# A higher schedule priority for VectorE's operations between attention scores and the softmax

## The chip, the core and the metric

The kernel runs on one core of a Trainium2 chip. The metric is the device time of one execution in microseconds (us). TensorE is written PE, VectorE DVE, ScalarE ACT, GpSimd POOL, SyncE (which issues most transfers) SP.

## What is computed

Two layers of a hybrid decoder over 512 tokens of width 1024, all in float32. Each layer normalises its input, projects it with one matrix to eight parts, runs a gated linear recurrence (HGRN2) on one half and sliding-window attention with sinks on the other, gates both and projects back:

```python
h = rms_norm(x, g_pre)
q_h, f_h, i_h, z_h, q_a, k_a, v_a, z_a = split(h @ w_in)
o_h = rms_norm(hgrn2(q_h, f_h, i_h, lb), g_head) * silu(z_h)
o_a = sliding_window_attention(rotary(q_a), rotary(k_a), v_a, sinks) * silu(z_a)
x   = x + rms_norm(concat(o_h, o_a) @ w_out, g_post)
```

Attention has 16 query heads of 64 and 2 key/value heads. A block of 128 queries sees 128 keys back, so two key blocks. The softmax has one more term, the head's sink, in its denominator:

```python
s = where(mask, einsum('bnqkgd,bnskd->bnkgqs', qb, kw) * ATT_SCALE, NEG_INF)
p = softmax(concat([s, sink]))[..., :-1]
o = einsum('bnkgqs,bnskd->bnqkgd', p, vw)
```

## The kernel before

**Projections.** Weights come from HBM in pieces of 128x512 floats (SP, line 161). Each piece is split into a high part `whi` (a cast on ACT, line 181) and a low part `wlo` (a subtraction, mostly on DVE, line 182), and each product of the projections is three matmuls (L293): high by low, low by high, high by high, added up in one of three PSUM banks `pj`. `step()` emits three such matmuls at a time. It also emits conversions ahead of their use by a table of due steps; nine buffers hold converted pieces.

**Attention** is a second stream. `merge` interleaves it with the projection steps by weights, so that a piece of attention follows every few steps. It goes through 16 steps (four groups `g` of four heads by four query blocks `n`). A step starts with `att_scores`; `att_transpose` follows for the step two before, and `att_value` for the step four before. In `att_scores`:

- PE computes scores into a bank `sc`: one bank and eight matmuls for `n == 0` (L556), else two banks with four matmuls each (L567).
- DVE masks them in place (L559, or L571 for each bank), takes the maximum over keys (L560, or L572 for each bank), joins it with the sink to the negated maximum `negm` (L575) and computes the sink's difference `ds` (L577).
- ACT takes four exponentials with `negm` as bias, one per head, and their sums (L581), and one of `ds` (L584).
- DVE adds and inverts the sums (L585, L586); POOL multiplies (L588).

`att_transpose` turns the probabilities on PE into a bank `sc` (L594) and splits them into a high and a low part (ACT L339, DVE L340); POOL cuts them into two key blocks with `affine_select` (L606). `att_value` multiplies them with the values (PE L620, ACT L622, DVE L626). Three banks `sc` go round among scores and transposes (`SC = 3`): a score matmul may start when the exponentials, or L340, have read what its bank held. The rotation of queries also runs in this stretch: DVE L510 to L517 from the projection's bank, POOL L520 and L521, ACT L526, DVE L527, then a store and a load of the group's queries (SP L529 and L500).

**Order.** A scheduler orders each engine's instructions at build time: by when it takes them to be ready, and among ready ones by a priority that follows program order. `pin(...)` keeps pinned instructions in program order; the score matmuls are pinned, the operations on DVE here are not. `tc.high_priority(n)` makes what is emitted inside count as emitted n places earlier. Each engine's queue then runs in its built order, and an instruction that waits holds up all behind it.

Of the kernel before, what the change touches and what calls it, by code (L numbers as in the profile page):

```python
# [14 lines left out]
ALU = mybir.AluOpType  # L15
AX = mybir.AxisListType
# [8 lines left out]
SCALE = 1.0 / np.sqrt(64.0)  # L25
# [45 lines left out]
def hybrid_kernel(ctx: ExitStack, tc: tile.TileContext, x, wkv, win, wout, g_pre, g_post, lbp, ghead, sinks,  # L71
                  gcol_c, cos_f, sin_f, cos_t, sin_t, masks_c, out):
    nc = tc.nc
    P = 128
# [9 lines left out]
    def pin(ins):  # L84
        return tc.keep_in_program_order(ins)
# [8 lines left out]
    def sc():  # L94
        sc_turn[0] += 1
        return sc_tiles[sc_turn[0] % SC]
# [5 lines left out]
    def tmp(tag, dt=F32, n=1):  # L102

        t = tp.tile([P, n, 512] if n > 1 else [P, 512], dt, tag=tag, name=tag, bufs=TB[tag])
        return t
# [337 lines left out]
    def layer(l, last):  # L443
# [98 lines left out]
        am4 = amask.unsqueeze(1).broadcast_to([P, 4, P])  # L542
        am2 = amask.unsqueeze(1).broadcast_to([P, 2, P])

        def att_scores(g, n):
            v = g // 2
            q = qs[g]
            hs = slice(4 * g, 4 * g + 4)
            t_ = slice(n * P, (n + 1) * P)
            mx_ = sm.tile([P, 4], F32, tag="mx", name="mx")  # L550
            cur = []
            if n == 0:
                S = sc()
                for h in range(4):
                    for p in range(2):
                        pin(nc.tensor.matmul(S[:, h * P:(h + 1) * P], lhsT=q[:, h, t_], rhs=kst[v][p][:, 0:P],  # L556
                                         start=(h == 0 and p == 0), stop=(h == 3 and p == 1)))
                Sv = S.rearrange("p (h s) -> p h s", h=4)
                nc.vector.copy_predicated(Sv, am4, neg.unsqueeze(2).broadcast_to([P, 4, P]))  # L559
                nc.vector.tensor_reduce(mx_, Sv, axis=AX.X, op=ALU.max)  # L560
                cur = [Sv[:, h, :] for h in range(4)]
            else:
                for hp_ in range(2):
                    S = sc()
                    for h in range(2):
                        for p in range(2):
                            pin(nc.tensor.matmul(S[:, h * 256:(h + 1) * 256], lhsT=q[:, 2 * hp_ + h, t_],  # L567
                                             rhs=kst[v][p][:, (n - 1) * P:(n + 1) * P],
                                             start=(h == 0 and p == 0), stop=(h == 1 and p == 1)))
                    Sv = S.rearrange("p (h s) -> p h s", h=2)  # L570
                    nc.vector.copy_predicated(Sv[:, :, P:2 * P], am2, Sv[:, :, 0:P])  # L571
                    nc.vector.tensor_reduce(mx_[:, 2 * hp_:2 * hp_ + 2], Sv[:, :, P:2 * P], axis=AX.X, op=ALU.max)  # L572
                    cur += [Sv[:, h, P:2 * P] for h in range(2)]
            negm = sm.tile([P, 4], F32, tag="negm", name="negm")
            nc.vector.scalar_tensor_tensor(negm, mx_, -SCALE, nsnk[:, l, hs], op0=ALU.mult, op1=ALU.min)  # L575
            ds_ = sm.tile([P, 4], F32, tag="ds", name="ds")
            nc.vector.tensor_tensor(ds_, snk[:, l, hs], negm, op=ALU.add)  # L577
            pt = tmp("s")
            sums = sm.tile([P, 4], F32, tag="sums", name="sums")
            for h in range(4):  # L580
                nc.scalar.activation(pt[:, h * P:(h + 1) * P], cur[h], AF.Exp, bias=negm[:, h:h + 1], scale=SCALE,  # L581
                                     accum_out=sums[:, h:h + 1])
            es = sm.tile([P, 4], F32, tag="es", name="es")
            nc.scalar.activation(es, ds_, AF.Exp)  # L584
            nc.vector.tensor_tensor(sums, sums, es, op=ALU.add)  # L585
            nc.vector.reciprocal(sums, sums)  # L586
            pv = pt.rearrange("p (h s) -> p h s", h=4)
            nc.gpsimd.tensor_tensor(pv, pv, sums.unsqueeze(2).broadcast_to([P, 4, P]), op=ALU.mult)  # L588
            return pt
# [38 lines left out]
        def att_stream(steps):  # L628


            pts, terms = {}, {}
            n = len(steps)
            for tt in range(NT):
                ensure(("k", l, tt))
            for i in range(n + VLAG):
                todo = []
                if i < n:
                    todo.append(lambda: pts.update({i: att_scores(*steps[i])}))
                if 2 <= i <= n + 1:
                    todo.append(lambda: terms.update({i - 2: att_transpose(*steps[i - 2], pts.pop(i - 2), i % 2)}))  # L640
                if i >= VLAG:
                    todo.append(lambda: att_value(*steps[i - VLAG], terms.pop(i - VLAG)))
                for fn in todo:
                    fn()
                    yield (SLOW[1] if i < SLOW[0] else 1.0) / len(todo)

                if i < n and steps[i][1] == NT - 1 and steps[i][0] < 2:
                    until(lambda: steps[i][0] + 2 in stacks)
                    load_q(steps[i][0] + 2)
# [431 lines left out]
    neg = const.tile([P, 1], F32, name="neg")  # L1081
    gh = const.tile([P, DEPTH], F32, name="gh")
    snk = const.tile([P, DEPTH, ATT_HEADS], F32, name="snk")
    nsnk = const.tile([P, DEPTH, ATT_HEADS], F32, name="nsnk")
# [95 lines left out]
```

## Time and profile before

| | us |
|---|---|
| median of 3 runs | 920.47 (920.27 to 921.49) |
| the profiled execution | 920.82 |
| its span, first to last instruction | 919.1 |

| engine | busy us | share of the span |
|---|---|---|
| PE, matmuls | 903.7 | 98% |
| PE, weight loads | 751.6 | 82% |
| DVE | 668.2 | 73% |
| ACT | 464.2 | 51% |
| POOL | 273.7 | 30% |

TensorE's granted clock was 0.999. Attention lies at about 60 to 165 us in layer 0 and 513 to 620 us in layer 1. A row of the timeline gives start, duration, engine, line, operation, tiles and count; in square brackets stands the idle time before it and who ended it. A line of the waits gives who waited for whom: microseconds in total, times, and the longest. In names, buffer numbers are left out. The shares are averages over the whole span; the stretches differ.

### The profile page before, as it was taken

The numbers are of one execution on the slowest core, as the hardware profiler recorded it, in microseconds if no ns is written. First come the engines' busy times: TensorE is split into PE (matmuls) and PEld (weight loads), VectorE is DVE, ScalarE is ACT, GpSimd is POOL, SyncE is SP. The second block draws the span as 40 slices with busy tenths as digits, with TensorE's granted clock in tenths as the row PEclk, the third lists the DMA queues.
The fourth block names the chain that finished last, engine by engine and source line by source line (L and its number), as shares of the span: only waits on it lengthen the run. The fifth ranks groups of instructions, "written<-read, shape, count | busy, mean of one in ns | idle before, by whom it ended". The sixth has DMA issues, their size and how long they took to land.

```text
span 919.1 us, 19004 instructions
## 1 busy us (share of the span) xinstructions
PE 903.7 (98%) x7240; PEld 751.6 (82%) x7240; DVE 668.2 (73%) x1326; ACT 464.2 (51%) x1100; POOL 273.7 (30%) x292
## 2 busy tenths in 40 slices
PE   8999999999999999999999999999999999999997
PEld 6888887888888888888888877888788888888885
DVE  5968877869854896655787689876889439866556
ACT  5535757652755422534464466686446463245242
POOL 3335443303413142121332254450134022330102
PEclk9999999999999999999999999999999999999999
DMA  6584612323222332333356557223322323213413
GB/s 225 184 241 135 166 38 86 92 84 102 71 70 69 121 99 73 92 103 115 116 165 190 161 148 173 58 70 92 94 71 82 93 78 95 82 47 93 138 35 137
DMA packets 56570, 100.74 MB, mean 110 GB/s; under 512 B 6560, under 2 KB 9120, under 8 KB 56480
## 3 DMA queue, kind: packets, MB, share of 16 engines
q1 hardware_dynamic: 56192, 99.40, 36.7%
q8 instruction: 57, 0.93, 0.4%
q14 instruction: 33, 0.27, 0.1%
q10 hardware_dynamic: 288, 0.14, 0.1%
HBM read 86.93 MB, written 12.58 MB: 108 GB/s over the span
## 4 chain that ended last, share of the span: by engine, by line
PE 88%; DVE 6%; ACT 2%; issue 1%; POOL 1%; DMA 0%; POOLq 0%; DVEq 0%; SPq 0%; ACTq 0%
PE pj L293 73%; PE sc L750 2%; PE sc L567 2%; PE ac L620 2%; PE ac L821 2%; DVE wlo L182 1%; PE ac L824 1%; PE ac L808 1%; ACT s L581 1%; PE sc L594 1%; PE sc L873 1%; PE sc L406 1%; PE sc L796 1%; DVE mx L572 0%; DVE a L340 0%
## 5 line engine op out<-in xcount | busy, mean ns | idle before, releaser
L182 DVE TENSOR_TENSOR wlo<-raw,whi 128x512 fp32r<-128x512 f32 x249 | 182.8, 748 | 51.4 <-ACT whi L181 50.6
L181 ACT CAST whi<-raw 128x512 fp32r<-128x512 f32 x256 | 154.2, 620 | 106.0 <-PE pj L293 92.7
L293 PE MATMUL pj<-hhi,wlo 128*128 128x512 f32 x512 | 203.7, 398 | 0.0
L293 PE MATMUL pj<-hhi,whi 128*128 128x512 f32 x512 | 199.7, 390 | 0.0
L293 PE MATMUL pj<-hlo,whi 128*128 128x512 f32 x512 | 199.5, 390 | 0.0
L293 PE MATMUL pj<-whi,ops 128*128 128x512 f32 (+1 forms) x520 | 172.5, 394 | 0.0
L293 PEld LDWEIGHTS pj<-hhi,whi 128*128 128x128 f32 x512 | 96.1, 188 | 20.7
L293 PEld LDWEIGHTS pj<-whi,ops 128*128 128x128 f32 x520 | 97.2, 188 | 19.3
L293 PEld LDWEIGHTS pj<-hhi,wlo 128*128 128x128 f32 x512 | 96.2, 188 | 19.1
L293 PEld LDWEIGHTS pj<-hlo,whi 128*128 128x128 f32 x512 | 96.3, 188 | 18.6
L293 PE MATMUL pj<-whi,hlo 128*128 128x512 f32 x256 | 103.5, 405 | 0.0
L293 PE MATMUL pj<-wlo,ops 128*128 128x512 f32 (+1 forms) x260 | 100.8, 388 | 0.0
L293 PE MATMUL pj<-wlo,hhi 128*128 128x512 f32 x256 | 100.4, 392 | 0.3 <-DVE wlo L182 0.2
L293 PE MATMUL pj<-whi,hhi 128*128 128x512 f32 x256 | 100.3, 392 | 0.0
L769 POOL TENSOR_TENSOR k<-k,tot 128x256 f32<-128x256 f32 x80 | 64.2, 832 | 107.1 <-PE sc L750 57.8
L581 ACT ACTIVATE s<-sc,negm 128x128 f32<-128x128 f32 x128 | 45.6, 368 | 38.7 <-DVE negm L575 38.7
L768 DVE TENSOR_TENSOR q<-q,tot 128x256 f32<-128x256 f32 x80 | 48.8, 648 | 12.7 <-PE sc L756 6.9
L293 PEld LDWEIGHTS pj<-whi,hhi 128*128 128x128 f32 x256 | 48.1, 188 | 10.2
L293 PEld LDWEIGHTS pj<-wlo,ops 128*128 128x128 f32 x260 | 49.0, 188 | 8.8
L293 PEld LDWEIGHTS pj<-wlo,hhi 128*128 128x128 f32 x256 | 48.3, 189 | 8.9 <-DVE wlo L182 1.0
L293 PEld LDWEIGHTS pj<-whi,hlo 128*128 128x128 f32 x256 | 48.2, 188 | 8.0
L588 POOL TENSOR_TENSOR s<-s,sums 128x512 f32<-128x512 f32 x32 | 34.1, 1067 | 44.3 <-DVE sums L586 28.6
(188 smaller groups left out, 1417.0 us busy)
## 6 DMA issues: line engine op xcount, KB each, us to landing
raw<-in_win_dram SPq DMA_DIRECT2D x192, 256.0 KB, 2.7
raw<-in_wout_dram SPq DMA_DIRECT2D x64, 256.0 KB, 2.7
stack<-rot SPq DMA_DIRECT2D x16, 512.0 KB, 3.4
qs<-stack SPq DMA_DIRECT2D x32, 256.0 KB, 4.7
a<-in_x_dram SPq DMA_DIRECT2D x12, 256.0 KB, 3.5
raw<-in_wkv_dram SPq DMA_DIRECT2D x8, 256.0 KB, 3.9
x_mid<-a SPq DMA_DIRECT2D x8, 256.0 KB, 2.8
a<-x_mid SPq DMA_DIRECT2D x8, 256.0 KB, 3.2
```

The source lines that it names most:

```text
L181: keep(nc.scalar.copy(hi, v))
L182: keep((nc.gpsimd if i in on_pool and i % 2 else nc.vector).tensor_tensor(lo, v, hi.bitcast(F32), op=ALU.subtract))
L293: nc.tensor.matmul(u.o, lhsT=u.sta(k, u.w)[i], rhs=u.mov(k, u.w)[j], start=(n == 0), stop=(n == len(u.list) - 1))
L406: pin(nc.tensor.transpose(o[:, j * P:(j + 1) * P], self.xn[:, c, j * P:(j + 1) * P], ident))
L567: pin(nc.tensor.matmul(S[:, h * 256:(h + 1) * 256], lhsT=q[:, 2 * hp_ + h, t_], rhs=kst[v][p][:, (n - 1) * P:(n + 1) * P], start=(h == 0 a ...
L581: nc.scalar.activation(pt[:, h * P:(h + 1) * P], cur[h], AF.Exp, bias=negm[:, h:h + 1], scale=SCALE, accum_out=sums[:, h:h + 1])
L588: nc.gpsimd.tensor_tensor(pv, pv, sums.unsqueeze(2).broadcast_to([P, 4, P]), op=ALU.mult)
L620: pin(nc.tensor.matmul(U, lhsT=vst[v][:, blk, :], rhs=d, start=(i == 0), stop=(i == len(terms) - 1)))
L750: pin(nc.tensor.matmul(L[32 * b:32 * b + 32, c:c + 16], lhsT=k[:, o_:o_ + 32], rhs=qv[:, blk:blk + qu, 1, :], start=True, stop=True, tile_ ...
L768: nc.vector.tensor_tensor(qv[:, :, 1, :], qv[:, :, 1, :], tv[:, :, 0].unsqueeze(2).broadcast_to([P, nb, hh]), op=ALU.mult)
L769: nc.gpsimd.tensor_tensor(kv_[:, :, 0, :], kv_[:, :, 0, :], tv[:, :, 1].unsqueeze(2).broadcast_to([P, nb, hh]), op=ALU.mult)
L821: pin(nc.tensor.matmul(O[:, c], lhsT=A[:, c], rhs=vs(j, n), start=(n == 0), stop=False))
```

## The change

Each of the six VectorE operations from the scores to the sink's difference is emitted with priority 300. No instruction is added or taken out, and no operand changes.

```diff
-                nc.vector.copy_predicated(Sv, am4, neg.unsqueeze(2).broadcast_to([P, 4, P]))
-                nc.vector.tensor_reduce(mx_, Sv, axis=AX.X, op=ALU.max)
+                with tc.high_priority(300):
+                    nc.vector.copy_predicated(Sv, am4, neg.unsqueeze(2).broadcast_to([P, 4, P]))
+                with tc.high_priority(300):
+                    nc.vector.tensor_reduce(mx_, Sv, axis=AX.X, op=ALU.max)
...
-                    nc.vector.copy_predicated(Sv[:, :, P:2 * P], am2, Sv[:, :, 0:P])
-                    nc.vector.tensor_reduce(mx_[:, 2 * hp_:2 * hp_ + 2], Sv[:, :, P:2 * P], axis=AX.X, op=ALU.max)
+                    with tc.high_priority(300):
+                        nc.vector.copy_predicated(Sv[:, :, P:2 * P], am2, Sv[:, :, 0:P])
+                    with tc.high_priority(300):
+                        nc.vector.tensor_reduce(mx_[:, 2 * hp_:2 * hp_ + 2], Sv[:, :, P:2 * P], axis=AX.X, op=ALU.max)
...
-            nc.vector.scalar_tensor_tensor(negm, mx_, -SCALE, nsnk[:, l, hs], op0=ALU.mult, op1=ALU.min)
+            with tc.high_priority(300):
+                nc.vector.scalar_tensor_tensor(negm, mx_, -SCALE, nsnk[:, l, hs], op0=ALU.mult, op1=ALU.min)
...
-            nc.vector.tensor_tensor(ds_, snk[:, l, hs], negm, op=ALU.add)
+            with tc.high_priority(300):
+                nc.vector.tensor_tensor(ds_, snk[:, l, hs], negm, op=ALU.add)
```

Lines shift: L559, L560, L571, L572, L575, L577 become L560, L562, L574, L576, L580, L583, and what follows moves by six (L581 is L587, L594 is L600, L626 is L632); L567 becomes L569. Below, numbers after a tile's name tell its bank (`sc_78` to `sc_80` are the three score banks). The order changes inside attention alone, in both layers. On PE it changes at five spots; on SP one weight load changes places with a query load in each layer.

*First place*, layer 0 at about 76 to 84 us, where the projection goes over to slab `IV`. DVE before:

```order
L340 TENSOR_TENSOR a<-sc_79,a 128x512
L517 TENSOR_TENSOR rot<-pj,cs 128x512
L571 COPY_PREDICATED sc_80<-masks,sc_80 128x2x128
L571 COPY_PREDICATED sc_78<-masks,sc_78 128x2x128
L572 TENSOR_REDUCE mx<-sc_80 128x2
L182 TENSOR_TENSOR wlo<-raw,whi 128x512
L572 TENSOR_REDUCE mx<-sc_78 128x2
L182 TENSOR_TENSOR wlo<-raw,whi 128x512 x2
L527 TENSOR_TENSOR rot<-rot 128x512 x2
L182 TENSOR_TENSOR wlo<-raw,whi 128x512
L575 SCALAR_TENSOR_TENSOR negm<-mx,nsnk 128x4
```

DVE now:

```order
L340 TENSOR_TENSOR a<-sc_79,a 128x512
L574 COPY_PREDICATED sc_80<-masks,sc_80 128x2x128
L574 COPY_PREDICATED sc_78<-masks,sc_78 128x2x128
L576 TENSOR_REDUCE mx<-sc_80 128x2
L576 TENSOR_REDUCE mx<-sc_78 128x2
L517 TENSOR_TENSOR rot<-pj,cs 128x512
L580 SCALAR_TENSOR_TENSOR negm<-mx,nsnk 128x4
L182 TENSOR_TENSOR wlo<-raw,whi 128x512
L583 TENSOR_TENSOR ds<-snk,negm 128x4
L182 TENSOR_TENSOR wlo<-raw,whi 128x512 x2
L527 TENSOR_TENSOR rot<-rot 128x512 x2
L182 TENSOR_TENSOR wlo<-raw,whi 128x512
```

The score operations and L517 now stand ahead of the first L182, and `negm` ahead of all four. ACT there, before and then now:

```order
L181 CAST whi<-raw 128x512 x3
L526 CAST rot<-rot 128x512 x2
L181 CAST whi<-raw 128x512
L339 CAST a<-sc_79 128x512
L657 COPY vt<-pj 128x512
L581 ACTIVATE s,sums<-sc_80,negm 128x128 x2
```

```order
L181 CAST whi<-raw 128x512 x2
L587 ACTIVATE s,sums<-sc_80,negm 128x128
L181 CAST whi<-raw 128x512
L526 CAST rot<-rot 128x512 x2
L181 CAST whi<-raw 128x512
L587 ACTIVATE s,sums<-sc_80,negm 128x128
```

The first exponential moved ahead of the third cast. In layer 1 ACT's order here is unchanged, and it had the exponential ahead of that cast before; on DVE only L517 moves behind the score operations there.

*Second place*, layer 0 at about 100 to 106 us, from group 1 to group 2; layer 1 moves alike. DVE before and then now:

```order
L182 TENSOR_TENSOR wlo<-raw,whi 128x512
L527 TENSOR_TENSOR rot<-rot 128x512 x2
L571 COPY_PREDICATED sc_79<-masks,sc_79 128x2x128
L571 COPY_PREDICATED sc_80<-masks,sc_80 128x2x128
L182 TENSOR_TENSOR wlo<-raw,whi 128x512
L572 TENSOR_REDUCE mx<-sc_79 128x2
L182 TENSOR_TENSOR wlo<-raw,whi 128x512
L572 TENSOR_REDUCE mx<-sc_80 128x2
L340 TENSOR_TENSOR a<-sc_78,a 128x512
L575 SCALAR_TENSOR_TENSOR negm<-mx,nsnk 128x4
```

```order
L574 COPY_PREDICATED sc_79<-masks,sc_79 128x2x128
L574 COPY_PREDICATED sc_80<-masks,sc_80 128x2x128
L576 TENSOR_REDUCE mx<-sc_79 128x2
L576 TENSOR_REDUCE mx<-sc_80 128x2
L182 TENSOR_TENSOR wlo<-raw,whi 128x512
L580 SCALAR_TENSOR_TENSOR negm<-mx,nsnk 128x4
L527 TENSOR_TENSOR rot<-rot 128x512
L583 TENSOR_TENSOR ds<-snk,negm 128x4
L527 TENSOR_TENSOR rot<-rot 128x512
L182 TENSOR_TENSOR wlo<-raw,whi 128x512 x2
L340 TENSOR_TENSOR a<-sc_78,a 128x512
```

Of three L182, two L527 and an L340 ahead of `negm`, one L182 is left. On PE, L556 of group 2 stands seven projection matmuls earlier, and six of these now stand between it and L594.

*Third place*, layer 0 at about 137 to 142 us; layer 1 moves alike. DVE before and then now:

```order
L571 COPY_PREDICATED sc_80<-masks,sc_80 128x2x128
L626 TENSOR_TENSOR oa<-ac_82,u 64x2x128
L182 TENSOR_TENSOR wlo<-raw,whi 128x512
L626 TENSOR_TENSOR oa<-ac_82,u 64x2x128
L572 TENSOR_REDUCE mx<-sc_80 128x2
L571 COPY_PREDICATED sc_78<-masks,sc_78 128x2x128
L182 TENSOR_TENSOR wlo<-raw,whi 128x512
L572 TENSOR_REDUCE mx<-sc_78 128x2
L340 TENSOR_TENSOR a<-sc_79,a 128x512
L575 SCALAR_TENSOR_TENSOR negm<-mx,nsnk 128x4
```

```order
L574 COPY_PREDICATED sc_80<-masks,sc_80 128x2x128
L632 TENSOR_TENSOR oa<-ac_82,u 64x2x128
L576 TENSOR_REDUCE mx<-sc_80 128x2
L574 COPY_PREDICATED sc_78<-masks,sc_78 128x2x128
L182 TENSOR_TENSOR wlo<-raw,whi 128x512
L576 TENSOR_REDUCE mx<-sc_78 128x2
L182 TENSOR_TENSOR wlo<-raw,whi 128x512
L580 SCALAR_TENSOR_TENSOR negm<-mx,nsnk 128x4
L632 TENSOR_TENSOR oa<-ac_82,u 64x2x128
L583 TENSOR_TENSOR ds<-snk,negm 128x4
L340 TENSOR_TENSOR a<-sc_79,a 128x512
```

L340 and the second half of the output sum (L626, now L632) fell behind `negm`.

## Prediction

> **What bounds the kernel now.** I read the page first, then who waited for whom, then the two attention stretches by windows, then the rows of single instructions.
>
> ```profile
> PE 903.7 (98%) x7240; PEld 751.6 (82%) x7240; DVE 668.2 (73%) x1326; ACT 464.2 (51%) x1100; POOL 273.7 (30%) x292
> PE 88%; DVE 6%; ACT 2%; issue 1%; POOL 1%; DMA 0%; POOLq 0%; DVEq 0%; SPq 0%; ACTq 0%
> ```
>
> TensorE (PE) is busy 98% of the span and makes 88% of the chain that ended last. An operation of VectorE (DVE) is worth time only where TensorE stands still for what follows from it. So the question is how long TensorE stands still in attention, and for whom.
>
> ```profile
> PEld sc L567 <- ACT s L581: 7.5, 16, 1.2
> PE sc L567 <- ACT s L581: 2.9, 5, 0.8
> ACT s L581 <- DVE negm L575: 38.7, 22, 6.3
> PE pj L293 <- DVE wlo L182: 0.2, 1, 0.2
> ```
>
> Read from below: a projection matmul (L293) waits for a weight's low part (wlo, L182) visibly once, for 0.2 us. The score matmuls (L567) wait 16 times for ScalarE's exponentials (L581), which must leave one of the three score banks first. The exponentials wait 22 times for the negated maximum (negm, L575), the end of the operations that get the priority.
>
> ```profile
> 105.00:120.00 15.00, 14.57 (x77) 11.69 (x76) 14.15 (x31) 9.62 (x36) 9.78 (x9) 1.00 0.79 181
> 135.00:150.00 15.00, 14.16 (x74) 11.24 (x72) 14.16 (x31) 11.02 (x36) 6.75 (x6) 1.00 0.36 98
> sum 105.00, PE 103.61 PEld 85.69 DVE 86.50 ACT 68.11 POOL 49.10; mean PE 14.80 PEld 12.24 DVE 12.36 ACT 9.73 POOL 7.01
> ```
>
> These are windows of layer 0's attention (length, then busy PE, PEld, DVE, ACT, POOL). Over 105 us DVE is busy 86.50, but where TensorE loses most, DVE is busy 14.15 and 14.16 of 15. There the order on DVE decides what is late. The visible idle, 105 - 103.61 = 1.4 us, is too small a sum: a matmul's row lasts longer than the step to the next one, so I take starts.
>
> ```profile
> 75.56 1.11 PE L567 MATMUL sc<-kst,qs 128*128 128x256 f32 x8
> 106.64 1.11 PE L556 MATMUL sc<-kst,qs 128*128 128x128 f32 x8
> 107.90 0.63 PE L594 MATMUL sc<-ident,s 128*128 128x128 f32 x4 [0.15 <-issue]
> 112.05 0.40 PE L293 MATMUL pj<-wlo,hhi 128*128 128x512 f32 x1
> 112.71 0.74 PE L567 MATMUL sc<-kst,qs 128*128 128x256 f32 x4 [0.27 <-ACT s L581]
> 117.64 1.41 PE L567 MATMUL sc<-kst,qs 128*128 128x256 f32 x8
> 141.38 0.39 PE L293 MATMUL pj<-hlo,whi 128*128 128x512 f32 x1
> 141.61 0.39 PE L293 MATMUL pj<-hhi,whi 128*128 128x512 f32 x1
> 142.79 1.44 PE L567 MATMUL sc<-kst,qs 128*128 128x256 f32 x8 [0.80 <-ACT s L581]
> 148.65 0.39 PE L293 MATMUL pj<-hhi,whi 128*128 128x512 f32 x1
> 149.08 1.45 PE L567 MATMUL sc<-kst,qs 128*128 128x256 f32 x8
> ```
>
> A projection matmul starts 0.23 after the last (141.38, 141.61), so 0.39 - 0.23 = 0.16 of each wait stays hidden. Eight score matmuls without a wait last 1.11. The stalls, with names for later: **P1** at 107.90, 0.15 + 0.16 = 0.31. **P2** at 112.71, 0.66 - 0.23 = 0.43. **P3** at 117.64, 1.41 - 1.11 = 0.30 (the second bank of the eight). **P4** at 142.79, 1.18 - 0.23 = 0.95, and 1.44 - 1.11 = 0.33 inside. **P5** at 149.08, 0.43 - 0.23 = 0.20, and 0.34 inside. Together 2.86 us; layer 1 has the same places 452.7 us later:
>
> ```profile
> 594.27 0.39 PE L293 MATMUL pj<-hhi,whi 128*128 128x512 f32 x1
> 595.45 1.44 PE L567 MATMUL sc<-kst,qs 128*128 128x256 f32 x8 [0.80 <-ACT s L581]
> ```
>
> P4 is again 1.18 - 0.23 = 0.95. Twice 2.86 = 5.7 us is all that this change can win.
>
> **The change, part by part.** No instruction is added or removed, so busy time on every engine stays; only waits move.
>
> *P4, the third place in the order.*
>
> ```profile
> 137.21 0.41 DVE L571 COPY_PREDICATED sc<-masks,sc 128x256 f32<-128x256 uint8 x1
> 137.53 0.40 DVE L626 TENSOR_TENSOR oa<-ac,u 64x256 f32<-64x256 f32 x1
> 139.54 0.43 DVE L572 TENSOR_REDUCE mx<-sc 128x2 f32<-128x256 f32 x1
> 140.21 0.69 DVE L182 TENSOR_TENSOR wlo<-raw,whi 128x512 fp32r<-128x512 f32 x1
> 141.15 0.68 DVE L340 TENSOR_TENSOR a<-sc,a 128x512 fp32r<-128x512 f32 x1
> 141.75 0.15 DVE L575 SCALAR_TENSOR_TENSOR negm<-mx,nsnk 128x4 f32<-128x4 f32 x1
> 141.93 0.37 ACT L581 ACTIVATE s<-sc,negm 128x128 f32<-128x128 f32 x1 [2.26 <-DVE negm L575]
> ```
>
> In the new order two L571, one L626, two L572 and two L182 stand before negm; L340 and the other L626 fall behind it. 2 x 0.41 + 0.40 + 2 x 0.43 + 2 x 0.69 = 3.46 from 137.21 gives 140.7 instead of 141.75: 1.1 earlier. TensorE wants the bank at 141.61 + 0.23 = 141.84 and got it 0.95 later, so this stall goes, and the 0.33 inside it: 1.28 won.
>
> *P5.* TensorE now comes 1.28 earlier. Between the sums of the step before and the next negm both orders hold the same amount (two L626, two operations of 0.69, the four score operations), so negm follows only the 1.1. P5 grows by 1.28 - 1.1 = 0.2. P4 and P5 together win 1.1; I take 1.0 for losses against GpSimd (POOL, below).
>
> *P1, P2, P3, the second place.*
>
> ```profile
> 105.39 0.15 DVE L575 SCALAR_TENSOR_TENSOR negm<-mx,nsnk 128x4 f32<-128x4 f32 x1
> ```
>
> Before it stood three L182, two L527, an L340; in the new order one L182. With the two L527, of L182's shape, at its 0.69, that is 4 x 0.69 + 0.68 = 3.4 earlier, so P1's bank is free. L556 of the next group stands seven matmuls (7 x 0.23 = 1.6 us) earlier on TensorE, so its maximum and exponentials can come 1.6 earlier against P2's 0.43 and P3's 0.30. I take all three as gone: 1.04.
>
> So 2.0 in each layer, 4.0 in all. Bounds: nothing (DVE is full there) and 5.7.
>
> *The first place.* Here the new order can cost time.
>
> ```profile
> 79.83 0.47 PE L293 MATMUL pj<-whi,hlo 128*128 128x512 f32 x1
> 80.43 0.50 PE L293 MATMUL pj<-wlo,hhi 128*128 128x512 f32 x1
> 78.94 2.04 DVE L182 TENSOR_TENSOR wlo<-raw,whi 128x512 fp32r<-128x512 f32 x2
> 78.09 1.74 POOL L521 TENSOR_TENSOR rot<-rot 128x512 f32<-128x512 f32 x1
> 64.16 1.29 POOL L521 TENSOR_TENSOR rot<-rot 128x512 f32<-128x512 f32 x1
> 531.87 0.50 PE L293 MATMUL pj<-wlo,hhi 128*128 128x512 f32 x1 [0.17 <-DVE wlo L182]
> 538.64 0.63 PE L567 MATMUL sc<-kst,qs 128*128 128x256 f32 x4
> 539.92 0.74 PE L567 MATMUL sc<-kst,qs 128*128 128x256 f32 x4 [0.65 <-ACT s L581]
> ```
>
> TensorE reads these weights as soon as they are made: it loses 0.60 - 0.23 = 0.37 at 80.43. The new order puts both L571, both L572 and L517 ahead of the first L182 here, and on ScalarE an exponential, which needs negm, ahead of the third cast. That is how layer 1 stands already before the change, and there this place costs 0.17 + 0.16 = 0.33 for the weight and 0.65 + 0.16 = 0.81 for the bank: 1.14. So layer 0 should lose 1.14 - 0.37 = 0.8. In layer 1 only L517 moves behind the score operations; L521 follows L517 and comes 4 x 0.4 = 1.6 later, beside the L182: between -0.3 and +0.8, I take 0.2, nearer to what layer 1 has.
>
> *What else moves.* L340, L626, L527 and L517 fall back by 1 to 3 us. L340's result is wanted on TensorE two steps later (one step is 149.08 - 142.79 = 6.3 us); L626 frees one of two accumulators; L517 a projection bank; the views name no wait of TensorE for any of the three. L527 feeds, through SP's queue, the queries of a group two groups on; behind it in that queue one weight load changes places with a query load. I cost these at nothing; without the cover each would cost its delay once. The other L182 are read later; the one visible wait of 0.2 us for a wlo says that they have room. If it is gone, that is the second rival.
>
> **Sum.** -4.0 + 0.8 + 0.2 = -3.0. The profiled execution took 920.82 (span 919.1), so 917.8; it lies 0.35 above the median of 920.47, against which it is 917.5. I say 917.7.
>
> **Rivals.** *DVE is simply full (no change).* P4 and P5 stay (1.8 per layer), P1 to P3 go (2.1 in all), the first place costs 0.8 in each layer: -0.5, about 920.3. For it: 14.16 of 15. Against it: L340 and L626 need not be done before negm. The Trainium skill ("Perfetto Trace Analysis", Optimization Strategy) holds that the same gap repeating on the engine that should be saturated can mean too little PSUM for the next tile. By that the three banks set the loss whatever the order, and the sum would be near zero; that P4 is 0.95 in both layers agrees, and the free 1.1 us before negm speaks against.
>
> *The weights come late (slower).* At the first place three conversions per layer are read at once. A DVE operation with two SBUF operands that meets a POOL operation waits for its end:
>
> ```profile
> 142.42 1.05 DVE L577 TENSOR_TENSOR ds<-snk,negm 128x4 f32<-128x4 f32 x1
> 141.91 1.55 POOL L606 TENSOR_SCALAR_AFFINE_SELECT pcur<-a 128x1024 fp32r<-128x1024 f32 x1 [3.39 <-DVE negm L575]
> ```
>
> Both end at 143.46 to 143.47. A turn lost to L521 costs 1.29 (its row at 64.16). Against 4.0 won, the kernel gets slower from the fourth lost turn (4 x 1.29 = 5.2) and measurably from the fifth; with all six it is 7.7 - 4.0 = 3.7 slower, 924.5. Against it: TensorE waits for one conversion at a time, and the next is made meanwhile. The Trainium skill ("SBUF — State Buffer", Who interferes with whom) says that VectorE with two SBUF inputs and a reading GpSimd lock each other out for whole instructions, the first to start winning; the trace agrees (0.15 us of work lasts 1.05). By that rule alone every meeting goes to whoever starts first, and L182 right after negm would start before L521 or lose the full 1.29.
>
> *The change does nothing* is out: the order shows the operations moved in both layers.
>
> **How the numbers follow.** 60% for the forecast, own range 915.6 (nearly all of 5.7 won, first place free) to 918.7. 28% for a full DVE, 918.7 to 922.2. 12% for late weights, above that. 0.2% (1.8 us) is about what a measurement of this kernel can tell from no change: faster is below 918.6, slower above 922.3. The range 915.6 to 921.2 leaves out the slower end and a little below. Faster 0.60, same 0.28, slower 0.12.
>
> **What would show it.** In the changed kernel's waits L567's lines for L581 should fall from 7.5 and 2.9 us by about half; near 142 and 595 the 0.80 should be gone; near 80 a wait for wlo or for L581 should appear that layer 0 did not have; exponentials should wait less than 38.7 us for negm. Wrong it would be if negm comes no earlier beside the L182, or if TensorE waits for wlo in more than one place per layer.

## Result and the profile after

The changed kernel takes 916.05 us (median of seven executions; all but the profiled one lie between 914.69 and 916.52) against 921.18 us for the kernel before on the same chip (920.27 to 921.79). The ratio is 0.9943 with a 95% interval of 0.9933 to 0.9953; by the medians it is 5.1 us less. The forecast was 917.7, with a range of 915.6 to 921.2. The sign came out as forecast; the gain is 1.7 times the 3.0 us of the sum. The profiled execution of these runs was disturbed (3166.89 us, the cause is not known), so the lines below come from a second set of the unchanged kernel, e1_after_again: 915.38 us, profiled execution 915.38, span 913.6.

The page of the changed kernel: busy time of the engines, and the chain that ended last.

```profile
PE 901.1 (99%) x7240; PEld 752.5 (82%) x7240; DVE 658.2 (72%) x1326; ACT 461.8 (51%) x1100; POOL 274.0 (30%) x292
PE 93%; DVE 4%; ACT 1%; issue 1%; POOL 1%; DMA 0%; POOLq 0%; DVEq 0%; ACTq 0%
```

The chain has lost a third of DVE's share (6% before) and half of ScalarE's (2%). DVE issues the same 1326 instructions, yet is busy 10.0 us less than before (668.2). I had written that busy time stays on every engine.

Who waited for whom in the changed kernel (us in all, times, longest). The lines have moved: L567 is now L569, L575 is L580, L577 is L583, L581 is L587, L594 is L600.

```profile
PEld sc L569 <- ACT s L587: 2.4, 10, 0.4
PE sc L569 <- ACT s L587: 0.4, 2, 0.2
PE pj L293 <- DVE wlo L182: 0.3, 1, 0.3
ACT s L587 <- DVE negm L580: 43.4, 23, 6.3
```

The score matmuls' waits fell from 7.5 to 2.4 and from 2.9 to 0.4. The one visible wait for a weight grew by 0.1. The last line went the other way than I said: ScalarE waits longer for negm, 43.4 against 38.7. In places it is through with its other work sooner and then stands idle: ahead of the exponentials of step 8 in layer 0 it was free at 110.91 before and is at 108.04 now, and they began at 111.15 and 109.63. An engine that isn't the bound may wait more in the faster kernel.

To see where the 5.5 us of the span went, I take the starts of the eight score matmuls of some steps. Steps are counted within a layer from 0; steps 1, 6, 11 and 15 bracket the first, second and third place. First the rows of before that the prediction has not shown, then those of the changed kernel.

```profile
62.91 1.11 PE L567 MATMUL sc<-kst,qs 128*128 128x256 f32 x8
92.71 1.11 PE L567 MATMUL sc<-kst,qs 128*128 128x256 f32 x8
124.37 1.11 PE L567 MATMUL sc<-kst,qs 128*128 128x256 f32 x8
514.54 1.10 PE L567 MATMUL sc<-kst,qs 128*128 128x256 f32 x8
545.28 1.12 PE L567 MATMUL sc<-kst,qs 128*128 128x256 f32 x8
577.03 1.12 PE L567 MATMUL sc<-kst,qs 128*128 128x256 f32 x8
601.74 1.44 PE L567 MATMUL sc<-kst,qs 128*128 128x256 f32 x8
```

```profile
62.78 1.12 PE L569 MATMUL sc<-kst,qs 128*128 128x256 f32 x8
92.72 1.12 PE L569 MATMUL sc<-kst,qs 128*128 128x256 f32 x8
116.70 1.45 PE L569 MATMUL sc<-kst,qs 128*128 128x256 f32 x8
123.44 1.12 PE L569 MATMUL sc<-kst,qs 128*128 128x256 f32 x8
140.90 1.12 PE L569 MATMUL sc<-kst,qs 128*128 128x256 f32 x8
146.66 1.42 PE L569 MATMUL sc<-kst,qs 128*128 128x256 f32 x8
512.00 1.10 PE L569 MATMUL sc<-kst,qs 128*128 128x256 f32 x8
542.22 1.12 PE L569 MATMUL sc<-kst,qs 128*128 128x256 f32 x8
572.94 1.12 PE L569 MATMUL sc<-kst,qs 128*128 128x256 f32 x8
596.16 1.40 PE L569 MATMUL sc<-kst,qs 128*128 128x256 f32 x8
```

The table gives the time from one of these starts to the next, in us, for every kernel of this study, from the same rows of each trace (1-6: step 1 to step 6). Each line is one execution; the two of the changed kernel agree within 0.05 us.

| kernel | layer 0: 1-6 | 6-11 | 11-15 | layer 1: 1-6 | 6-11 | 11-15 |
|---|---|---|---|---|---|---|
| before | 29.80 | 31.66 | 24.71 | 30.74 | 31.75 | 24.71 |
| changed (e1_after_again) | 29.94 | 30.72 | 23.22 | 30.22 | 30.72 | 23.22 |
| changed (e9_after_third) | 29.94 | 30.74 | 23.21 | 30.17 | 30.74 | 23.21 |
| e2_last_group | 29.83 | 31.63 | 23.22 | 30.95 | 31.70 | 23.22 |
| e3_second_place | 30.62 | 30.40 | 24.71 | 30.71 | 30.72 | 24.69 |
| e4_first_place | 29.95 | 31.74 | 24.69 | 30.22 | 31.70 | 24.70 |
| e5_negm_first | 29.94 | 30.44 | 23.22 | 30.30 | 30.38 | 23.22 |
| e6_rotary_early | 31.08 | 30.70 | 23.23 | 30.96 | 30.73 | 23.23 |
| e7_four_banks | 30.46 | 30.33 | 23.94 | 29.84 | 30.80 | 23.90 |
| e8_maxima_only | 30.10 | 30.87 | 23.35 | 30.19 | 31.00 | 23.33 |
| e10_negm_first_again | 29.95 | 30.43 | 23.22 | 30.33 | 30.45 | 23.22 |
| e11_ds_late | 30.19 | 30.45 | 23.22 | 30.19 | 30.43 | 23.24 |

Changed against before: first place +0.14 and -0.52, second -0.94 and -1.03, third -1.49 and -1.49. That is -5.33 of the 5.5; everything else together is under 0.2. So nothing is given back outside attention. The forecast had +0.8 and +0.2, -1.04 twice, and -1.0 twice.

### The profile page after: what moved, and what is told of

It reads as the page before. It is cut to its first block, busy times and chain, and to the rows that moved or that the text cites. A ratio compares the mean times of both kernels' runs of the same rounds, so it can differ in the third digit from the quotient of the medians.

```text
span 3165.2 us, 19010 instructions
## 1 busy us (share of the span) xinstructions
PE 3157.0 (100%) x7240; PEld 1846.9 (58%) x7240; DVE 662.1 (21%) x1326; ACT 470.1 (15%) x1100; POOL 266.2 (8%) x292
## 4 chain that ended last, share of the span: by engine, by line
PE 99%; issue 0%; DVE 0%; POOL 0%; ACT 0%; POOLq 0%; DVEq 0%; ACTq 0%
PE pj L293 82%; PE ac L626 3%; PE sc L569 2%; PE ac L827 2%; PE sc L600 2%; PE sc L756 2%; PE ac L814 1%; PE ac L830 1%; PE sc L406 1%; PE sc L879 1%; PE sc L556 1%; PE sc L802 1%; PE sc L767 0%; PE sc L490 0%; PE sc L762 0%
## 5 line engine op out<-in xcount | busy, mean ns | idle before, releaser
L293 PE MATMUL pj<-hhi,wlo 128*128 128x512 f32 x512 | 566.5, 1106 | 0.0
L293 PE MATMUL pj<-hhi,whi 128*128 128x512 f32 x512 | 560.7, 1095 | 0.0
L293 PE MATMUL pj<-hlo,whi 128*128 128x512 f32 x512 | 560.4, 1095 | 0.0
L293 PE MATMUL pj<-whi,ops 128*128 128x512 f32 (+1 forms) x520 | 512.7, 1091 | 0.0
L293 PEld LDWEIGHTS pj<-hlo,whi 128*128 128x128 f32 x512 | 222.8, 435 | 181.3 <-issue 179.8
L293 PEld LDWEIGHTS pj<-whi,ops 128*128 128x128 f32 x520 | 221.1, 427 | 180.6 <-issue 173.2
L182 DVE TENSOR_TENSOR wlo<-raw,whi 128x512 fp32r<-128x512 f32 x249 | 179.6, 726 | 535.9 <-ACT whi L181 535.3
L293 PE MATMUL pj<-whi,hlo 128*128 128x512 f32 x256 | 290.2, 1135 | 0.0
L293 PE MATMUL pj<-wlo,ops 128*128 128x512 f32 (+1 forms) x260 | 281.1, 1081 | 0.0
L293 PE MATMUL pj<-whi,hhi 128*128 128x512 f32 x256 | 280.3, 1095 | 0.0
L293 PE MATMUL pj<-wlo,hhi 128*128 128x512 f32 x256 | 279.1, 1092 | 0.0
L569 PEld LDWEIGHTS sc<-kst,qs 128*128 128x128 f32 x192 | 80.9, 465 | 19.5 <-issue 18.1
L569 PE MATMUL sc<-kst,qs 128*128 128x256 f32 x192 | 85.3, 680 | 0.0
```

The source lines that it names most:

```text
L182: keep((nc.gpsimd if i in on_pool and i % 2 else nc.vector).tensor_tensor(lo, v, hi.bitcast(F32), op=ALU.subtract))
L293: nc.tensor.matmul(u.o, lhsT=u.sta(k, u.w)[i], rhs=u.mov(k, u.w)[j], start=(n == 0), stop=(n == len(u.list) - 1))
```

## Experiments

Theory A is that of the forecast: negm comes earlier on DVE, the exponentials free the score banks earlier, and stalls of TensorE at named places go. Its rivals: the gain comes from elsewhere (B), what is left is ScalarE's pace (C), the weights come late (D), three banks set the loss whatever the order. Theory E concerns the first place: L517's place decides there whether negm loses a turn to GpSimd.

**e1_after_again: the change, unaltered.**

> The changed kernel itself, for a second set of times and a trace of it. Theory A (the forecast's mechanism: the exponentials get negm earlier and the stalls P1 to P5 of TensorE go): 4.6 to 5.6 us faster than before, as in its first set of times; the 0.80 and 0.65 of L567's waits are gone, negm's waits on ScalarE fall clearly below 38.7 us. Theory B (the gain comes from elsewhere, the other order of TensorE's rows or weights that are ready earlier): the same time, but L567's waits for L587 (which was L581) still sum to over 7 us and near 142 and 595 the stall of 0.95 stands.

Measured: 915.38 us against 921.08, ratio 0.9931 (0.9918 to 0.9943), 5.7 us less. The larger stalls are gone as A says, but negm's waits rose instead of falling; that indicator was wrong, not the theory. Theory B falls for the third place: at step 14 the matmuls run through (1.12 at 140.90, where before it was 1.44 after a wait of 0.80).

**e2_last_group, e3_second_place, e4_first_place: the three places one by one.** The edit stands at each of the six operations; the conditions are `>= 12`, `7 <= ... <= 11` and `== 3`.

```diff
-                with tc.high_priority(300):
+                with tc.high_priority(300) if 4 * g + n >= 12 else ExitStack():
```

> The priority in steps 12 to 15 of each layer alone (group 3, where P4 and P5 lie); TensorE's order is that of before. Theory A with the forecast's sizes (1.0 a layer, P5 grows while P4 goes): 2.0 us faster than before. Theory A with P4 and P5 both gone: 2 x 1.82 = 3.6 us faster. Theory B: within 0.5 us of before.

> The priority in steps 7 to 11 of each layer alone (negm of step 7, then group 2, where P1 to P3 lie). Theory A: 2 x 1.04 = 2.1 us faster than before. DVE simply full: within 0.5 us of before. If this and the priority in steps 12 to 15 alone add up to the whole gain of 5.1 us, the first place costs nothing.

> The priority in step 3 alone (the last of group 0), where TensorE reads weights as soon as they are made. The forecast's sizes: 0.8 us in layer 0 and 0.2 in layer 1, so 1.0 us slower than before. If the first place is free: within 0.3 us of before. Theory B (the gain comes from the order of TensorE's rows, which this step alone changes in layer 0): 2 us faster or more.

Measured against 921.08: e2 918.43, ratio 0.9967 (0.9954 to 0.9979); e3 919.75, ratio 0.9983 (0.9974 to 0.9992); e4 920.45, ratio 0.9990 (0.9981 to 0.9999). In us that is 2.65, 1.33 and 0.63 less, 4.6 in all, against 5.7 for the whole change on the same chip.

e2 lies between the two sizes expected; the table gives it -1.49 twice. P4 is gone and so is the 0.20 of P5, but the 0.3 inside the matmuls of step 15 stays. TensorE's order in e2 is that of before from end to end, so at the third place the gain is not TensorE's order but DVE's. e4 is a miss of the forecast: the place that was to cost 1.0 us wins. Its layer 1 is the cleanest of these runs: the orders of TensorE, ScalarE and GpSimd there are those of before, and on DVE the one difference is L517, which stands behind the four score operations. That alone wins 0.52. e3 shows -1.26 and -1.03 at its own place, and in layer 0 +0.82 at the first place, which it does not touch: every engine's order there is that of before. These rows tell why; the first two are from before, the others from e3.

```profile
84.59 0.16 DVE L585 TENSOR_TENSOR sums<-sums,es 128x4 f32<-128x4 f32 x1 [1.06 <-ACT es L584]
84.59 1.12 POOL L606 TENSOR_SCALAR_AFFINE_SELECT pprev<-a 128x1024 fp32r<-128x1024 f32 x1
```

```profile
84.23 1.11 DVE L591 TENSOR_TENSOR sums<-sums,es 128x4 f32<-128x4 f32 x1 [1.06 <-ACT es L590]
84.23 1.09 POOL L612 TENSOR_SCALAR_AFFINE_SELECT pprev<-a 128x1024 fp32r<-128x1024 f32 x1
89.17 0.74 PE L569 MATMUL sc<-kst,qs 128*128 128x256 f32 x4 [0.70 <-ACT s L587]
```

In both kernels a DVE operation with two SBUF operands and a GpSimd operation start at the same hundredth of a microsecond. In before DVE ran through and took 0.16; in e3 it ended only with GpSimd's operation and took 1.11. The next negm on DVE then stands at 87.43, 0.46 later than in before (86.97), and TensorE stood still for 0.70 at 89.17. So a part of the shortfall of e3's profiled execution is a turn that fell the other way. Its -1.26 is in turn a little flattered: TensorE came late to the second place, and negm of step 9 stands 1.34 us ahead of the matmuls of step 10, against 1.05 in the changed kernel.

**e5_negm_first: negm ahead of the weights.** In the changed kernel an L182 still stands between the last maximum and negm in steps 9 and 14, and an L632 in step 15.

```diff
+    def behind(ins):
+        if newest:
+            tc.add_manual_dep(ins.ins, newest[-1].ins.name, ...)
+        return ins
...
+            low = keep((nc.gpsimd if i in on_pool and i % 2 else nc.vector).tensor_tensor(...))
+            if not (i in on_pool and i % 2):
+                behind(low)
...
+        behind(nc.vector.tensor_tensor(lo, src, hi.bitcast(F32), op=ALU.subtract))
...
+                newest.append(nc.vector.scalar_tensor_tensor(negm, ...))
```

> The changed kernel, and on DVE no L182 and no L340 that is written behind a negm may stand ahead of it. TensorE's order is that of the changed kernel; on DVE it differs at two places in each layer, both where an L182 had slipped between the last maximum and negm (steps 9, 14 and 15). Theory A (negm's place sets what is left of P3 and P5): negm comes 0.60 earlier at 115.65 and 145.59, the 0.32 and 0.30 that are left inside the eight score matmuls go, 2 x 0.62 = 1.2 us faster than the changed kernel, 6.5 to 7.0 faster than before. Theory C (what is left is the pace of the exponentials, two of them 0.69 against four matmuls of 0.12 each, whenever negm comes): as fast as the changed kernel, 5.2 to 5.7 faster than before. Theory D (the weights, now behind negm, come late): slower than the changed kernel, with a wait for wlo near 115 or 146.

Measured: 914.57 against 921.02, ratio 0.9928 (0.9916 to 0.9941). The negm of step 9 (here L590) and the score matmuls (L579) of steps 10 and 15:

```profile
115.68 0.16 DVE L590 SCALAR_TENSOR_TENSOR negm<-mx,nsnk 128x4 f32<-128x4 f32 x1
117.23 1.11 PE L579 MATMUL sc<-kst,qs 128*128 128x256 f32 x8
146.91 1.11 PE L579 MATMUL sc<-kst,qs 128*128 128x256 f32 x8
```

The changed kernel has 1.45 and 1.42 in these two places. Its negm stood 1.05 us ahead of the matmuls (115.65 and 116.70), here it stands 1.55 ahead, and the stall inside is gone. Theory C falls: two exponentials do take longer than four matmuls, but with negm half a microsecond earlier the second bank is free in time too. D falls as well: no wait for wlo at these places. TensorE's one visible wait for a wlo, at the first place of layer 1, grew from 0.3 to 0.5.

**e6_rotary_early: L517 ahead of the scores again.**

```diff
-                nc.vector.tensor_tensor(b[:, 1], o, cosf, op=ALU.mult)
+                with tc.high_priority(600):
+                    nc.vector.tensor_tensor(b[:, 1], o, cosf, op=ALU.mult)
```

> The changed kernel, with L517 (the second half of the rotary products, which releases GpSimd's L521) put ahead of the score operations again. TensorE's and ScalarE's orders are those of the changed kernel. Theory E (the first place won because L517 fell behind the maxima, so that negm starts before L521 and the turn lost to GpSimd falls on ds): negm meets L521 again, lasts about 1.0 instead of 0.15 in layer 1, the stall of 0.35 near 536 returns to 0.8, and 0.5 to 1.5 us of the gain are lost. Forecast's step (L521 beside the conversions is what costs): with L521 out of the way of the L182, the waits for wlo of 0.37 near 80 and 0.51 near 529 go, and the kernel is 0.5 to 0.9 us faster than the changed one.

Measured: 916.69 against 921.02, ratio 0.9956 (0.9943 to 0.9968). That is 0.9 to 1.3 us above the changed kernel's medians in the other sets (915.82 and 915.38), as E has it. The forecast's step falls: the waits for wlo did not go (two visible ones, 0.6 us in all). The table: +1.14 and +0.74 at the first places against the changed kernel, the other four as there. For layer 1, negm and its neighbour on GpSimd in before, in the changed kernel, and in e6:

```profile
529.99 1.02 DVE L575 SCALAR_TENSOR_TENSOR negm<-mx,nsnk 128x4 f32<-128x4 f32 x1
529.72 1.28 POOL L521 TENSOR_TENSOR rot<-rot 128x512 f32<-128x512 f32 x1
```

```profile
527.39 0.15 DVE L580 SCALAR_TENSOR_TENSOR negm<-mx,nsnk 128x4 f32<-128x4 f32 x1
527.58 1.29 DVE L583 TENSOR_TENSOR ds<-snk,negm 128x4 f32<-128x4 f32 x1
527.55 1.30 POOL L521 TENSOR_TENSOR rot<-rot 128x512 f32<-128x512 f32 x1 [0.34 <-DVE negm L580]
536.84 0.74 PE L569 MATMUL sc<-kst,qs 128*128 128x256 f32 x4 [0.19 <-ACT s L587]
```

```profile
529.18 1.01 DVE L581 SCALAR_TENSOR_TENSOR negm<-mx,nsnk 128x4 f32<-128x4 f32 x1
529.14 1.04 POOL L595 TENSOR_TENSOR s<-s,sums 128x512 f32<-128x512 f32 x1
539.31 0.75 PE L570 MATMUL sc<-kst,qs 128*128 128x256 f32 x4 [0.63 <-ACT s L588]
86.31 1.10 DVE L581 SCALAR_TENSOR_TENSOR negm<-mx,nsnk 128x4 f32<-128x4 f32 x1
86.31 1.09 POOL L613 TENSOR_SCALAR_AFFINE_SELECT pprev<-a 128x1024 fp32r<-128x1024 f32 x1
89.08 0.74 PE L570 MATMUL sc<-kst,qs 128*128 128x256 f32 x4 [0.88 <-ACT s L588]
```

In before negm lost 0.9 us to L521. In the changed kernel L517 stands behind the maxima, so L521 starts 0.16 after negm, and ds pays instead. In e6 negm lasts 1.01 again and the bank's stall is back at 0.63 visible. That confirms E in its effect; the GpSimd operation that negm met is the probabilities' product (L595), not L521, since L521 was done by then. The path from this negm to the bank goes through ScalarE, whose exponentials of step 3 stand among the casts of weights. With a late negm the casts are late, and DVE waits for them; in before:

```profile
532.19 0.69 DVE L182 TENSOR_TENSOR wlo<-raw,whi 128x512 fp32r<-128x512 f32 x1 [0.37 <-ACT whi L181]
533.06 0.69 DVE L182 TENSOR_TENSOR wlo<-raw,whi 128x512 fp32r<-128x512 f32 x1 [0.17 <-ACT whi L181]
```

In e6 these two waits are 0.59 and 0.17; in the changed kernel and in e4 there are none. The maximum and negm of the next step stand behind them on DVE, and that negm sets when step 5's second bank is free.

Layer 0, which before had no such stall, now has 0.88. Most of that is not L517's doing but another turn: at 86.31 negm of step 4 and a GpSimd operation start together, and negm takes 1.10, against 0.28 in the changed kernel. The profiled execution of e6 is the slowest of its five (918.35; the others 916.54 to 917.65), so layer 0's +1.14 says little about L517.

**e7_four_banks: more banks, without the priority.** With one accumulator the two transposes of the norm's gains at the start share a bank, so values differ from there on (and so do other pairs of accumulators further on); the instructions stay the same.

```diff
-PJ, SC = 3, 3
+PJ, SC = 3, 4
```

> The kernel before, without the change, with four score banks and one accumulator for the values instead of three and two. Rival on the banks (three banks set the stalls, whatever the order): L567's waits for L581 and P1 to P5 go, up to 5.7 us less, against a new wait of the values' matmuls (L620) for their one accumulator. Theory A: a fourth bank takes P1 to P5 away too, since a bank then has a step more to come free, but that says nothing on the order; the one accumulator costs more than it wins: at least one wait of 0.5 us in each of 16 steps in both layers, so 5 to 15 us slower than before.

Measured: 936.37 us, ratio to before 1.0162 (1.0148 to 1.0176), 15 us slower. The values' matmuls (L620), which I had named as the loser, wait visibly only twice, both times after the last scores of a layer; most of the cost comes in the later stage that uses the same accumulators:

```profile
PE ac L808 <- DVE q L831: 7.7, 8, 1.1
PE ac L821 <- DVE q L831: 4.0, 4, 1.1
PE ac L620 <- DVE oa L626: 3.3, 2, 1.7
```

In attention the fourth bank does help: 30.33 and 30.80 at the second place, 23.94 and 23.90 at the third, without the priority. At the third place no engine's order differs from before, so 0.8 there is the bank's alone; at the second the scheduler has moved rows on TensorE and DVE too, so that figure is not. At the first place layer 1 wins 0.90 and layer 0 loses 0.66; the six stretches together are 4.1 us shorter. So an additional bank and an earlier negm both shorten the same stalls. What the rival claimed beyond that, that three banks set the loss whatever the order, falls: with three banks the new order reaches 23.22 at the third place.

**e8_maxima_only: priority for the copies and maxima, not for negm and ds.** The edit takes the two `with` lines off L580 and L583.

> The priority on the copies and maxima alone (L560, L562, L574, L576), not on negm and ds. At the first place negm then stands behind the L182 and L527 as before the change; at the second it stands behind two L527 and two L182 more than in the changed kernel; at the third behind one L626 more. Theory A (negm's own place is what counts): the first place and P1 win nothing, P4 goes as in the changed kernel: 2.5 to 3.5 us faster than before. If the earlier maxima were what counts: 4.6 to 6 us, as the whole change.

Measured: 916.47 against 921.02, ratio 0.9946 (0.9933 to 0.9960), 4.55 less. I expected 2.5 to 3.5 and was wrong: the maxima alone bring most of it, though negm then has two L527 and two L182 more ahead of it at the second place. P1 is gone there, and so is P3, which the whole change leaves: negm of step 9 stands 1.99 us ahead of the matmuls of step 10. What stays is P2, which the whole change takes away:

```profile
112.43 0.74 PE L569 MATMUL sc<-kst,qs 128*128 128x256 f32 x4 [0.29 <-ACT s L587]
```

That P1 is gone is not negm's doing in this run: negm of step 7 stands 1.14 us ahead of step 8's scores (L556), no more than before (1.25). But TensorE's order has moved too, and three projection matmuls stand between L556 and the transposes (L600, which was L594), where before there was none.

The table has 30.87 and 31.00 at the second place against 30.72, and +0.30 against before at the first place of layer 0. In layer 1 the first place wins as in the whole change (30.19): the maxima are what pushes L517 back, as E says.

**e9_after_third, e10_negm_first_again, e11_ds_late: side by side.** e10 is e5's kernel; e11 takes the `with` off ds (L583) in it.

> The changed kernel again, beside the two that follow: 915.4 to 916.0 us, 5.2 to 5.7 us faster than before.

> The kernel with negm ahead of every L182 and L340 that is written behind it, again, now beside the changed kernel. By places its first trace wins 1.2 us over the changed kernel (0.6 at the second place, 0.6 inside the matmuls of step 15), by its times 0.8. Theory A: 0.8 to 1.2 us faster than the changed kernel. If the two agree within 0.3 us, what was won at those places is given back elsewhere.

> The same kernel with ds (L583) back at its own place in the schedule. In layer 0's first place three L182 then follow each other behind negm, ahead of ds, which had lost 1.26 us there to GpSimd's L521 between the first and the second L182. If ds is what makes the weight late: the wait for wlo near 80.7 goes, 0.4 us faster. If the turn is lost by whichever operation comes next: the second L182 waits for L521's end instead, the wait of 0.36 stays, as fast as with ds early (within 0.3 us).

Measured against 921.47: e9 915.82, ratio 0.9937 (0.9924 to 0.9951); e10 914.89, ratio 0.9929 (0.9917 to 0.9942); e11 914.75, ratio 0.9928 (0.9916 to 0.9941). e10 is 0.9 us faster than the changed kernel beside it, as theory A has it, though the intervals overlap; by places it is 0.31 and 0.29 at the second place and about 0.3 inside step 15 in each layer. It and e11 are the fastest orders found, equal within their intervals. e11 tells who loses a turn. Its rows at the first place of layer 0:

```profile
78.80 2.39 DVE L190 TENSOR_TENSOR wlo<-raw,whi 128x512 fp32r<-128x512 f32 x2
78.29 1.75 POOL L531 TENSOR_TENSOR rot<-rot 128x512 f32<-128x512 f32 x1 [0.33 <-DVE negm L590]
```

With ds out of the way, the next conversion (L182, here L190) waits for the end of GpSimd's operation in its stead, and the time is the same (0.24 more at the first place of layer 0, 0.14 less in layer 1). TensorE's wait for that weight is hidden in the rows; from start to start it is 0.31 against 0.37 in e10. It is not ds that makes the weight late.

## Why the prediction was right, and where its sizes were off

**Right: the places, and the mechanism where it could be isolated.** The sum rested on P1 to P5, and e2 and e3 alone bring -1.49 twice and -1.26 and -1.03 at just those places. At the third place e2 shows DVE's order to be the cause, and e5 does so for P3 and for what was left in step 15. At P1 and P2 the change moves TensorE's order as well, and no run moves DVE's alone; there the mechanism is argued, and e8 loses P1 without an earlier negm.

That the second place came out at -0.94 and -1.03 against -1.04 is in part luck. P1 and P2 went, 0.74 as priced, but P3 stayed (1.45 at 116.70), because negm still had an L182 ahead of it; e5 removed it. In layer 0 the missing 0.30 was made up to 0.2 by starts beside the stalls that the sum had not counted: 0.12 ahead of L556 at 106.64 and 0.10 behind the matmul at 112.71. In layer 1 P2 was 0.53 and not 0.43. Late weights, the slow rival, did not come about.

**Mis-sized: the third place, 1.0 a layer against 1.49 measured.** The step that failed is the 3.46 us from the first L571 to negm. I added the rows' durations. I had corrected TensorE's rows for their overlap, but not DVE's: there too a row lasts longer than the step to the next one.

```profile
136.28 0.41 DVE L574 COPY_PREDICATED sc<-masks,sc 128x256 f32<-128x256 uint8 x1
136.60 0.40 DVE L632 TENSOR_TENSOR oa<-ac,u 64x256 f32<-64x256 f32 x1
139.12 0.15 DVE L580 SCALAR_TENSOR_TENSOR negm<-mx,nsnk 128x4 f32<-128x4 f32 x1
145.59 0.16 DVE L580 SCALAR_TENSOR_TENSOR negm<-mx,nsnk 128x4 f32<-128x4 f32 x1
```

From 136.28 to 136.60 is 0.32, not 0.41. The seven operations took 139.12 - 136.28 = 2.84. Before, the way was 141.75 - 137.21 = 4.54, so negm gained 1.70 and not 1.1. With that P5 does not grow by 0.2: the next negm stands 146.66 - 145.59 = 1.07 ahead of the matmuls that want the bank, and the 1.05 of before (148.03 to 149.08) is just met.

**Mis-sized, with the wrong sign: the first place, +1.0 against -0.38.** The step was the analogy: layer 0 would come to stand as layer 1 stood before, at 1.14. But layer 1's 0.81 hung on L517 standing ahead of the scores, which made negm meet GpSimd; the change moves L517 behind them in both layers. e4 shows it: with L517 moved and nothing else in layer 1, the stall is 0.33, and 0.36 and 0.35 is what the changed kernel has in layers 0 and 1. So layer 0 did get a new stall, as forecast, but less than half of the one priced. The weight's part of the step held: the wait for wlo is still 0.37 in layer 0, and in layer 1 it grew from 0.33 to 0.51. e6, which puts L517 back, stands at +1.28 and +0.22 against before. That this resembles the forecast's +0.8 and +0.2 is chance: layer 0's figure holds the turn lost at 86.31, and the forecast's +0.2 was for L517 behind the scores. Rows of the old order priced the old order, not the new one.

**Wrong, without weight in the sum: "busy time on every engine stays".** The same operations by groups (count, busy us, mean ns), before and after:

```profile
L577 DVE TENSOR_TENSOR ds<-snk,negm 128x4 f32<-128x4 f32 x32 | 17.7, 553 | 0.7
L182 DVE TENSOR_TENSOR wlo<-raw,whi 128x512 fp32r<-128x512 f32 x249 | 182.8, 748 | 51.4 <-ACT whi L181 50.6
```

```profile
L583 DVE TENSOR_TENSOR ds<-snk,negm 128x4 f32<-128x4 f32 x32 | 11.8, 369 | 0.8
L182 DVE TENSOR_TENSOR wlo<-raw,whi 128x512 fp32r<-128x512 f32 x249 | 179.4, 736 | 51.0 <-ACT whi L181 50.6
```

Waiting for GpSimd is booked as busy time. ds and L182 alone are busy 9.3 us less, with nothing removed; a turn of this kind is not on any list of waits. The Trainium skill ("SBUF — State Buffer", Who interferes with whom) has the rule that whichever issues first holds the shared port for its whole instruction. The rows of before (POOL at 529.72, negm at 529.99) and of e11 agree. The turns at 84.23 and 86.31 can neither bear it out nor refute it, since both rows start together.

The Trainium skill's rule on repeating gaps ("Perfetto Trace Analysis", Optimization Strategy), that they can mean too little PSUM for the next tile, agrees in part: at the third place a fourth bank wins 0.8 us a layer (e7), but an earlier release wins 1.49 with three.

**Open.** What share DVE's and TensorE's orders have in P1 and P2 was not separated. Whether the 0.35 us that TensorE still waits between the two banks of step 5 in either layer can be won was not tried. How much of the run-to-run spread comes from turns such as those at 84.59 and 84.23 was not measured.

## What to carry to other kernels

When a full engine works for the bound engine, look at the order on it before its load: here six small operations in front of the rest were worth 5 us, and most of it came from the four that fill the maximum. Price a new order by start-to-start steps of every engine in it, and take no price from a row whose neighbours the change also moves. A short operation with a long row beside a GpSimd operation is a lost turn: count it as a wait.

## What the runs showed of the hardware that I had not expected

A turn lost to GpSimd can hang on less than the profile's hundredth of a microsecond: two operations that start together at 84.59 in one kernel and at 84.23 in another end in opposite order, 0.16 against 1.11 us, and the matmuls five microseconds on show it with 0.70 of idle time. Among the 128x4 operations of attention the traces hold three more such ties: in e2 (84.07) and e8 (85.24) DVE ran through in 0.16, in e6 (86.31) it took 1.10. In nanoseconds the traces put DVE's start 1 to 3 ahead of GpSimd's in all five, the two that it lost included, so at this scale the recorded starts do not tell who wins.
